# Fifty-one series of extra products in one group of layer 0, at other addresses, orders and widths

## The chip, the cores and the metric

The kernel runs on one core of a Trainium2 chip. The metric is the device time of one execution in microseconds; a smaller time is better. Times of before are the median of two runs, and one further execution was profiled.

## The reference

A small decoder with two layers works on 16 learned prefix tokens and 256 input tokens, T = 272 in all, with a model width of 2048 and a hidden width of 8192. Layer 0 mixes tokens by forgetting attention, layer 1 by stick-breaking attention; after each mixer comes an MLP, and the change lies in that of layer 0:

```python
def squared_relu_mlp(h, w_up, w_down):
    u = h @ w_up
    return jnp.square(jax.nn.relu(u)) @ w_down
...
        h = h + squared_relu_mlp(rms_norm(h, norm_mlp[layer]), w_up[layer], w_down[layer])
```

Only the 256 input tokens are returned, so layer 1 carries 256 columns where layer 0 carries 272.

## The kernel before

Activations are kept feature-major: 128 features on the partitions, tokens along the free dimension. Every weight matrix is cut into groups of 512 output features. A group (`gemm_group`, line 179) has four accumulators in PSUM (`acc`, one for 128 output features each) and runs over four blocks of 512 input features. A block comes in two halves: each is loaded by the queue of SyncE into a tile `raw`, ScalarE copies it into the high part `whi` (line 220), and VectorE subtracts to get the low part `wlo` (line 221). The pools for `raw`, `whi` and `wlo` have four buffers each, which is two blocks.

The activations are split in the same way into a high and a low part (`Split`, line 101). For each chunk of 128 input features and each accumulator there are three products: high weights with high rows, high with low, low with high. In each, 128 columns of weights are the stationary operand and the 272 (or 256) columns of one activation row are the moving operand. All are issued by one helper, `gemm_matmul`, whose products therefore all stand under line 168. It can tie a product to the one before it, so that the order on TensorE is the order of the program.

Places in SBUF are chosen: in layer 0 an activation row starts 192 bytes behind a multiple of 256 bytes (`ROWS`), and the 128 columns of weights at a multiple of 256 bytes. In layer 1 the rows start at a multiple of 256 bytes and the weights 64 bytes behind one, and in some groups three products read 6 columns more (`widen`).

The MLP (`mlp`, line 550) has four quarters f of the hidden width; each has four groups g of `w_up` and then four of `w_dn`. The group of the change is f = 0, g = 1 of layer 0, the 18th group of the program. Its normed rows are called `x_m`, its accumulators `acc`; block 2 is its third. In blocks 1 and 2 the products run through the first half for all four accumulators, then through the second.

A second PSUM pool, `patt` (line 48), has four banks for everything that is not a group's accumulator: scores, transposes, sums of norms. At the start of the program nine products into a tile `idle` of that pool are made while the first loads arrive (line 64); no instruction reads that tile.

Of the kernel before, what the change touches and what calls it, by code (L numbers as in the profile page):

```python
# [9 lines left out]
F32 = mybir.dt.float32  # L10
# [5 lines left out]
P = 128  # L16
# [4 lines left out]
T = M + S  # L21
# [13 lines left out]
def yoco_kernel(ctx: ExitStack, tc: tile.TileContext, hT_in, gains, b_f, w_f, w_qkv0, w_o0, w_up, w_dn,  # L35
# [12 lines left out]
    patt = ctx.enter_context(tc.tile_pool(name="patt", bufs=4, space=bass.MemoryType.PSUM))  # L48
# [117 lines left out]
    def gemm_matmul(*args, **kw):  # L166

        ins = nc.tensor.matmul(*args, **kw).ins  # L168
        if queued and pinned[0]:
            tc.add_manual_dep(ins, queued[0].name, mybir.DependencyInfo(mybir.DependencyClass.NoSync,  # L170
                                                                        mybir.DependencyReason.DATA))
        queued[:] = [ins]
# [3 lines left out]
        tc.add_manual_dep(ins.ins, queued[0].name, mybir.DependencyInfo(mybir.DependencyClass.NoSync,  # L176
                                                                        mybir.DependencyReason.DATA))

    def gemm_group(wblk, sp, t0, evac, before={}, after={}, load_x=None, widen=False):

        uid[0] += 1
        u = uid[0]
        accs = [pacc.tile([P, 512], F32, tag="acc", name=f"acc_{u}_{m}") for m in range(4)]
        n = T - t0
        for kb in range(4):
            src_w = wblk[kb].rearrange("p (k c) -> p k c", k=4)  # L190
            if kb in before:
                before[kb]()
            piece = 1 if load_x is not None and kb < 2 else 2
            raws = [wraw.tile([P, 2, 512], F32, tag="raw", name=f"raw_{u}_{kb}_{hf}") for hf in range(2)]
            for k0 in range(0, 4, piece):
                if load_x is not None:
                    load_x(range(4 * kb + k0, 4 * kb + k0 + piece))
                if load_x is not None and kb == k0 == 0:

                    for c0 in (0, 256):  # L200
                        nc.scalar.dma_start(raws[0][:, 0, c0:c0 + 256], src_w[:, 0, c0:c0 + 256])
                else:
                    nc.sync.dma_start(raws[k0 // 2][:, k0 % 2:k0 % 2 + piece], src_w[:, k0:k0 + piece])
            parts = []
            for hf in range(2):
                whi = wspl.tile([P, 2 * 576], F32R, tag="whi", name=f"whi_{u}_{kb}_{hf}")
                wlo = wspl.tile([P, 2, 576], F32R, tag="wlo", name=f"wlo_{u}_{kb}_{hf}")
                if t0:
                    whi = whi.rearrange("p (k c) -> p k c", k=2)[:, :, 16:528]
                    wlo = wlo[:, :, 16:528]  # L210
                else:
                    whi = whi[:, :1024].rearrange("p (k c) -> p k c", k=2)
                    wlo = wlo[:, :, :512]
                boxes = [(o, piece, 0, 512) for o in range(0, 2, piece)]
                if load_x is not None and kb == hf == 0:
                    boxes[:1] = [(0, 1, 0, 256), (0, 1, 256, 512)]
                for o, no, c0, c1 in boxes:
                    src = raws[hf][:, o:o + no, c0:c1]
                    hp, lp = whi[:, o:o + no, c0:c1], wlo[:, o:o + no, c0:c1]
                    on_act = nc.scalar.activation(hp, src, AF.Copy)  # L220
                    on_dve = nc.vector.tensor_tensor(out=lp, in0=src, in1=hp.bitcast(F32), op=ALU.subtract)  # L221
                parts.append((whi, wlo))
            if kb in after:
                with tc.issue_after(on_act.ins), tc.issue_after(on_dve.ins):
                    after[kb]()


            if load_x is not None and kb == 0:
                runs = [([kc], range(4)) for kc in range(4)]
            elif kb in (0, 3):  # L230
                runs = [(range(4), [m]) for m in range(4)]
            else:
                runs = [(range(2 * hf, 2 * hf + 2), range(4)) for hf in range(2)]
            pinned[0] = load_x is None
            for kcs, ms in runs:
                if t0:
                    series = [(w, x, kc, m) for w, x in ((0, "hi"), (0, "lo"), (1, "hi")) for m in ms for kc in kcs]
                else:
                    series = [(w, x, kc, m) for m in ms for kc in kcs for w, x in ((0, "hi"), (0, "lo"), (1, "hi"))]
                for i, (w, x, kc, m) in enumerate(series):  # L240
                    over = SPAN if widen and kb == m == 0 and i in (0, 4, 8) else 0
                    rhs = sp.wide[x] if over else getattr(sp, x)[:, 4 * kb + kc]
                    gemm_matmul(accs[m][:, :n + over], parts[kc // 2][w][:, kc % 2, m * P:(m + 1) * P], rhs,
                                start=kb == kc == w == 0 and x == "hi", stop=kb == kc == 3 and w == 1)
                if kb == 3:
                    for m in ms:
                        evac(m, accs[m][:, :n])

    def residual_add(c, acc, t0):
        nc.vector.tensor_tensor(out=hT[:, c, t0:], in0=acc, in1=hT[:, c, t0:], op=ALU.add)  # L250
# [6 lines left out]
    def load_x(chunks):  # L257
        c0, n = chunks[0], len(chunks)
        nc.sync.dma_start(hT[:, c0:c0 + n, :], hT_in[:, c0:c0 + n, :])
        if c0 == 0:  # L260
            nc.sync.dma_start(g_sb, gains)
        for c in chunks:
            split_chunk(xa, G_A0, c)

    def first_norm(kb):
        if kb == 1:
            box["wf"] = load_gates()
        for c in range(4 * kb, 4 * kb + 4):
            norm.add(c)
# [173 lines left out]
    for g in range(4):  # L443
# [6 lines left out]
        if g == 0:  # L450

            gemm_group(w_qkv0[0], xa, 0, lambda m, acc, qT=qT: nc.scalar.copy(qT[:, m, :], acc),
                       after={kb: (lambda kb=kb: first_norm(kb)) for kb in range(4)}, load_x=load_x)
# [96 lines left out]
    def mlp(layer, xm, norm, t0, last_evac):  # L550
        box = {}

        def get_rstd():
            box["r"] = norm.finish()

        for f in range(N_FF):
            u = Split(f"u{layer}_{f}", t0)
            for g in range(4):
                def evac(m, acc, g=g):
                    c = 4 * g + m  # L560
                    r = tmp.tile([P, T], F32, tag="relu", name=f"relu_{layer}_{f}_{c}")
                    u2 = tmp.tile([P, T], F32, tag="u2", name=f"u2_{layer}_{f}_{c}")
                    nc.vector.scalar_tensor_tensor(out=r[:, t0:], in0=acc, scalar=0.0, in1=box["r"][:, t0:],
                                                   op0=ALU.max, op1=ALU.mult)
                    nc.scalar.activation(u2[:, t0:], r[:, t0:], AF.Square)
                    nc.scalar.activation(u.hi[:, c], u2[:, t0:], AF.Copy)
                    nc.vector.tensor_tensor(out=u.lo[:, c], in0=u2[:, t0:], in1=u.hi[:, c].bitcast(F32),
                                            op=ALU.subtract)
                gemm_group(w_up[layer, f, g], xm, t0, evac, {2: get_rstd} if f == g == 0 else {},
                           widen=t0 == M and g % 2 == 1)  # L570
            for g in range(4):
                def evac(m, acc, g=g):
                    residual_add(4 * g + m, acc, t0)
                    if f == N_FF - 1:
                        last_evac(4 * g + m)
                gemm_group(w_dn[layer, f, g], u, t0, evac, widen=t0 == M and g % 2 == 1)
# [20 lines left out]
    for g in range(4):  # L597
# [4 lines left out]
        def split_c(kb, g=g):  # L602
            for c in ([4 * kb + g - 1] if g < 3 else [4 * kb + 2, 4 * kb + 3]):
                split_chunk(xc, G_KV, c)

        gemm_group(w_q1[g], xq, M, evac_q1, {2: get_rstd1} if g == 0 else {},
                   after={kb: (lambda kb=kb: split_c(kb)) for kb in range(4)} if g else {}, widen=g > 0)
# [3 lines left out]
    for g in range(4):  # L611
# [4 lines left out]
        s, e, r = (att.tile([P, 4, 416], F32, tag="s", bufs=3, name=f"{t}1_{g}") for t in ("s", "e", "r"))  # L616
# [49 lines left out]
    def last_evac(c):  # L666
        if c < NC - 4:
            normf.add(c)
        else:
            if c == NC - 4:  # L670
                add_squares(normf.acc, True, False)
            sq = tmp.tile([P, T], F32, tag="sq", name=f"sq_fin_{c}")
            nc.scalar.activation(sq[:, M:], hT[:, c, M:], AF.Square)
            add_squares(sq, False, c == NC - 1)
        if c < NC - 4:
            nc.scalar.activation(hT[:, c, M:], hT[:, c, M:], AF.Copy, scale=g_sb[:, G_FIN, c:c + 1])
# [3 lines left out]
    a, y, t, rs = (fin[:, i, :] for i in range(4))  # L680
# [9 lines left out]
    for i in range(2):  # L690
        pr = patt.tile([P, 512], F32, tag="patt", name=f"pr_fin_{i}")
        for b in range(2):
            nc.tensor.matmul(pr[:, b * P:(b + 1) * P], rs[:, b:b + 1].to_broadcast([P, P]), ident,
                             start=True, stop=True)
# [67 lines left out]
```

## Time and profile before

| | us |
|---|---|
| median of the runs (2276.69 and 2277.55) | 2277.12 |
| the profiled execution | 2277.15 |
| its span, first to last instruction | 2275.4 |
| PE busy | 2262.0 |
| DVE busy | 1361.6 |
| ACT busy | 1113.5 |

PE is TensorE's products, PEld its weight loads, DVE is VectorE, ACT ScalarE, POOL GpSimd, and SP the queue of SyncE. L168 is line 168 of the kernel. A product's duration in the profile runs from its start to its modelled end and overlaps that of the next, so the pace of a stream is read from starts or from the number of products in a stretch. Names in the profile leave out buffer numbers. A float32 product has two rows in the profile, and one in lower precision (float32r, as in the groups) has one.

### The profile page before, as it was taken

What the parts mean: (1) busy time and instruction counts of PE and PEld (TensorE: products, weight loads), DVE (VectorE), ACT (ScalarE), POOL (GpSimd) and SP (SyncE); (2) the same over time, 40 slices, a digit from 0 to 9 for tenths busy, and PEclk for the clock granted to TensorE, in tenths of its full rate; (3) what the DMA queues carried; (4) which work ended last, traced back from release to release, by engine and by line L of the source; (5) the groups of instructions that cost most, each with busy time, mean ns of one, the idle gap of its engine ahead of it and who ended that gap; (6) DMA issues with size and microseconds to landing.
All of it is one profiled execution on the core that took longest, in us unless ns stands there. A gap on an engine that the chain in (4) does not pass through costs nothing.

```text
span 2275.4 us, 44753 instructions
## 1 busy us (share of the span) xinstructions
PE 2262.0 (99%) x18882; PEld 2255.5 (99%) x18882; DVE 1361.6 (60%) x1915; ACT 1113.5 (49%) x1536; POOL 28.5 (1%) x75
## 2 busy tenths in 40 slices
PE   9999999999999999999999999999999999999998
PEld 9999999999999999999999999999999999999998
DVE  7767676555454455445666677766555555555554
ACT  6554554443354344344454567655544443544553
POOL 0000000000000000000000000000000000000000
PEclk9999999999999999999999999999999999999999
DMA  7545554555555555555565544455656656556563
GB/s 241 174 162 168 182 168 160 184 179 173 186 170 185 179 170 186 172 185 179 170 192 183 180 160 157 159 187 189 199 187 193 203 187 201 191 188 202 184 204 130
DMA packets 116905, 412.32 MB, mean 181 GB/s; under 512 B 13520, under 2 KB 16992, under 8 KB 116704
## 3 DMA queue, kind: packets, MB, share of 16 engines
q1 hardware_dynamic: 114560, 406.29, 54.7%
q8 instruction: 148, 2.42, 0.4%
q10 hardware_dynamic: 2144, 3.17, 0.4%
q14 instruction: 53, 0.43, 0.1%
HBM read 407.29 MB, written 2.11 MB: 180 GB/s over the span
## 4 chain that ended last, share of the span: by engine, by line
PE 98%; DMA 1%; DVE 0%; ACT 0%; issue 0%; ACTq 0%; SPq 0%; DVEq 0%
PE acc L168 96%; PE po L414 1%; PE ps L345 0%; DMA fk<-f_dram 0%; PE po L417 0%; PE ps L343 0%; DMA raw<-w_qkv 0%; PE po L418 0%; PE pf L293 0%; DVE ob L704 0%; ACTq L319 0%; DVE s L471 0%; PE pms_fin L661 0%; DVE ob L701 0%; ACT x_o L438 0%
## 5 line engine op out<-in xcount | busy, mean ns | idle before, releaser
L221 DVE TENSOR_TENSOR wlo<-raw,whi 128x1024 fp32r<-128x1024 f32 (+1 forms) x773 | 926.5, 1215 | 664.6 <-ACT whi L220 657.2
L220 ACT ACTIVATE whi<-raw 128x1024 fp32r<-128x1024 f32 (+1 forms) x773 | 797.0, 1051 | 934.9 <-PE acc L168 904.8
L168 PE MATMUL acc<-x_u,whi 128*128 128x272 f32 (+1 forms) x4096 | 642.9, 281 | 0.0
L168 PE MATMUL acc<-x_m,whi 128*128 128x272 f32 (+1 forms) x4096 | 642.5, 281 | 0.0
L168 PEld LDWEIGHTS acc<-x_u,whi 128*128 128x128 f32 x4096 | 565.8, 188 | 0.0
L168 PEld LDWEIGHTS acc<-x_m,whi 128*128 128x128 f32 x4096 | 565.7, 188 | 0.0
L168 PE MATMUL acc<-x_u,wlo 128*128 128x272 f32 (+1 forms) x2048 | 440.8, 281 | 0.0
L168 PE MATMUL acc<-x_m,wlo 128*128 128x272 f32 (+1 forms) x2048 | 440.7, 281 | 0.0
L168 PE MATMUL acc<-x_a,whi 128*128 128x272 f32 (+1 forms) x2048 | 353.2, 285 | 0.7 <-ACT whi L220 0.7
L168 PEld LDWEIGHTS acc<-x_u,wlo 128*128 128x128 f32 x2048 | 323.3, 188 | 0.0
L168 PEld LDWEIGHTS acc<-x_m,wlo 128*128 128x128 f32 x2048 | 323.3, 188 | 0.0
L168 PEld LDWEIGHTS acc<-x_a,whi 128*128 128x128 f32 x2048 | 300.0, 188 | 2.2 <-ACT whi L220 1.2
L168 PE MATMUL acc<-x_a,wlo 128*128 128x272 f32 (+1 forms) x1024 | 253.1, 285 | 0.9 <-DVE wlo L221 0.9
L168 PE MATMUL acc<-x_kv,whi 128*128 128x272 f32 x1024 | 192.6, 287 | 0.0
L168 PEld LDWEIGHTS acc<-x_a,wlo 128*128 128x128 f32 x1024 | 175.5, 188 | 2.0 <-DVE wlo L221 1.6
L168 PE MATMUL acc<-x_o,whi 128*128 128x272 f32 (+1 forms) x1024 | 162.5, 282 | 0.7 <-ACT x_o L438 0.4
L168 PEld LDWEIGHTS acc<-x_kv,whi 128*128 128x128 f32 x1024 | 160.1, 188 | 0.0
L168 PE MATMUL acc<-x_kv,wlo 128*128 128x272 f32 x512 | 147.1, 287 | 0.0
L168 PEld LDWEIGHTS acc<-x_o,whi 128*128 128x128 f32 x1024 | 142.0, 188 | 1.4 <-DVE x_o L439 0.7
L250 DVE TENSOR_TENSOR hT<-acc,hT 128x272 f32<-128x272 f32 (+1 forms) x160 | 69.0, 431 | 86.4 <-PE acc L168 86.2
L168 PE MATMUL acc<-x_o,wlo 128*128 128x272 f32 (+1 forms) x512 | 110.5, 282 | 0.0
L168 PEld LDWEIGHTS acc<-x_kv,wlo 128*128 128x128 f32 x512 | 96.5, 188 | 0.0
(187 smaller groups left out, 1053.4 us busy)
## 6 DMA issues: line engine op xcount, KB each, us to landing
raw<-w_up SPq DMA_DIRECT2D x256, 512.0 KB, 4.5
raw<-w_dn SPq DMA_DIRECT2D x256, 512.0 KB, 4.5
raw<-w_qkv SPq DMA_DIRECT2D x92, 512.0 KB, 4.0
raw<-w_o SPq DMA_DIRECT2D x64, 512.0 KB, 4.5
raw<-w_kv SPq DMA_DIRECT2D x64, 512.0 KB, 4.6
raw<-w_q SPq DMA_DIRECT2D x32, 512.0 KB, 4.6
fk<-f_dram ACTq DMA_DIRECT2D x4, 544.0 KB, 6.4
raw<-w_qkv SPq DMA_DIRECT2D x7, 256.0 KB, 4.5
```

The source lines that it names most:

```text
L168: ins = nc.tensor.matmul(*args, **kw).ins
L220: on_act = nc.scalar.activation(hp, src, AF.Copy)
L221: on_dve = nc.vector.tensor_tensor(out=lp, in0=src, in1=hp.bitcast(F32), op=ALU.subtract)
L250: nc.vector.tensor_tensor(out=hT[:, c, t0:], in0=acc, in1=hT[:, c, t0:], op=ALU.add)
L414: ins = nc.tensor.matmul(po[:, i, :], v[:, j, 0, :], p[:, j, :2 * P], start=i == 0, stop=False)
```

## The change

A new helper, `probes`, makes 51 series of products and is called once: in layer 0, in group f = 0, g = 1, after the weights of block 2 have been split and before the products of that block. It takes the first half of the block. The moving operand is read from the high part `whi` (`wa`, 1024 columns in one run), the stationary one is 128 columns of the low part `wlo` (`wb`). Each series writes one tile `push` of the pool `patt`: its first product starts the sum, its last ends it, and no instruction reads it. The result of the kernel doesn't depend on it.

- 28 series of 32 products: from one product to the next the start of the moving operand goes on by `dx` pieces of 64 bytes and that of the weights by `dw`, each modulo four pieces; dx = dw = 0 is left out.
- 8 series of 20: 17 pieces of 16 columns, with a step of 48 or of 32 columns between the pieces, from four starting places.
- 4 series of 20 that read 272 columns backwards, one by one, and 4 that read 17 pieces of 16 columns in backward order.
- 2 series of 20 with the weights at 40 or 24 columns, and 5 with 264, 276, 280, 288 and 304 columns instead of 272.

```diff
+    def probes(parts, u):
+
+        (wa, wb), _ = parts
+        wa, wb = wa.rearrange("p k c -> p (k c)"), wb[:, 0]
+        near = lambda k: wb[:, 16 * k:16 * k + P]
+        row = lambda k, n=T: wa[:, 16 * k:16 * k + n]
+        lines = lambda o, step, n: bass.AP(wa.tensor, wa.offset + o, [wa.ap[0], [step, n], [1, 16]])
+        kinds = []
+        for dx in range(4):
+            for dw in range(4):
+                e = (dx - dw) % 4
+                for first in ((0, 1, 2, 3) if e == 0 else (0, 1) if e == 2 else (0,)):
+                    if dx or dw:
+                        kinds.append((32, [(row((first + i * dx) % 4), near(i * dw % 4)) for i in range(4)]))
+        for step in (48, 32):
+            for k in range(4):
+                kinds.append((20, [(lines(16 * k, step, 17), near(0))]))
+        for k in range(4):
+            kinds.append((20, [(bass.AP(wa.tensor, wa.offset + 16 * k + T - 1, [wa.ap[0], [-1, T]]), near(0))]))
+        for k in range(4):
+            kinds.append((20, [(lines(16 * k + T - 16, -16, 17), near(0))]))
+        for o in (40, 24):
+            kinds.append((20, [(row(3), wb[:, o:o + P])]))
+        for n in (264, 276, 280, 288, 304):
+            kinds.append((20, [(row(3, n), near(0))]))
+        for i, (n, pairs) in enumerate(kinds):
+            t = patt.tile([P, 512], F32, tag="patt", name=f"push_{u}_{i}")
+            for k in range(n):
+                x, w = pairs[k % len(pairs)]
+                c = 1
+                for _, m in x.ap[1:]:
+                    c *= m
+                gemm_matmul(t[:, :c], w, x, start=k == 0, stop=k == n - 1)
...
+            if probe and kb == 2:
+                probes(parts, u)
+
             if load_x is not None and kb == 0:
...
                 gemm_group(w_up[layer, f, g], xm, t0, evac, {2: get_rstd} if f == g == 0 else {},
+                           probe=layer == 0 and f == 0 and g == 1,
                            widen=t0 == M and g % 2 == 1)
```

On TensorE in the program before, at the end of block 1 of that group and the start of block 2 (`acc_0` to `acc_3` are the group's accumulators, `whi_1_1` is the high part of block 1, second half, `whi_2_0` that of block 2, first half; the last column is the output's shape and how often the row repeats):

```order
L168 MATMUL acc_3_5326<-x_m_3910,whi_1_1_5395 128x272 x2
L168 MATMUL acc_3_5326<-x_m_3910,wlo_1_1_5396 128x272
L168 MATMUL acc_0_5323<-x_m_3910,whi_2_0_5451 128x272 x2
L168 MATMUL acc_0_5323<-x_m_3910,wlo_2_0_5452 128x272
...
L168 MATMUL acc_1_5324<-x_m_3910,whi_2_0_5451 128x272 x2
```

The two rows ahead of the first product into `acc_0` are the last of block 1. In the changed program the same place on TensorE begins so, with the first three of the 51 series:

```order
L168 MATMUL acc_3_5326<-x_m_3910,whi_1_1_5395 128x272 x2
L168 MATMUL acc_3_5326<-x_m_3910,wlo_1_1_5396 128x272
L168 MATMUL push_0_5459<-whi_2_0_5451,wlo_2_0_5452 128x272 x32
L168 MATMUL push_1_5492<-whi_2_0_5451,wlo_2_0_5452 128x272 x32
L168 MATMUL push_2_5525<-whi_2_0_5451,wlo_2_0_5452 128x272 x32
```

The series follow block 1 directly. And it ends so, with the four widest series and the first product of block 2 into `acc_0`:

```order
L168 MATMUL push_47_6782<-whi_2_0_5451,wlo_2_0_5452 128x276 x20
L168 MATMUL push_48_6803<-whi_2_0_5451,wlo_2_0_5452 128x280 x20
L168 MATMUL push_49_6824<-whi_2_0_5451,wlo_2_0_5452 128x288 x20
L168 MATMUL push_50_6845<-whi_2_0_5451,wlo_2_0_5452 128x304 x20
L168 MATMUL acc_0_5323<-x_m_3910,whi_2_0_5451 128x272 x2
```

The 1356 products stand in one run between the two blocks; nothing else on TensorE changes its place, and VectorE, ScalarE, GpSimd and SyncE have the same instructions in the same order as before.

More of the change, by code (lines that the diff above doesn't have):

```diff
@@ L177, in behind, with gemm_group @@
                                                                         mybir.DependencyReason.DATA))
-    def gemm_group(wblk, sp, t0, evac, before={}, after={}, load_x=None, widen=False):
+    def probes(parts, u):
[30 more added lines that the diff above has]
+                gemm_matmul(t[:, :c], w, x, start=k == 0, stop=k == n - 1)
+    def gemm_group(wblk, sp, t0, evac, before={}, after={}, load_x=None, widen=False, probe=False):
         uid[0] += 1
```

## The prediction

> **What bounds the kernel now.** The first view is the page: busy times, the granted clock in 40 slices, and the chain that ended last.
>
> ```profile
> PE 2262.0 (99%) x18882; PEld 2255.5 (99%) x18882; DVE 1361.6 (60%) x1915; ACT 1113.5 (49%) x1536; POOL 28.5 (1%) x75
> PEclk9999999999999999999999999999999999999999
> PE 98%; DMA 1%; DVE 0%; ACT 0%; issue 0%; ACTq 0%; SPq 0%; DVEq 0%
> ```
>
> TensorE is busy for 2262.0 of 2275.4 us, the granted clock never drops, and the chain that ends last lies to 98% on PE. So a product added on PE has nothing to hide behind: it moves the end by the time until the next product can start. PEld, the weight loads, is as full as PE; each product of this kernel brings its own weight load.
>
> That time is not the mean of the groups by line (281 to 288 ns): consecutive products overlap, so the step from start to start has to be read. Two views give it: the windows, over long stretches that hold nothing but products of line 168, and the timeline at the place of the change.
>
> ```profile
> 470.00:930.00 460.00, 460.00 (x3732) 1.00 0.55 179
> 1500.00:2200.00 700.00, 700.00 (x6176) 1.00 0.60 193
> ```
>
> The columns are the stretch, its length, PE's busy time with the number of products, granted clock, DMA share and GB/s. The first stretch is layer 0, 272 columns a product: 460.00/3732 = 123.3 ns a step. The second is layer 1 with 256 columns (a few with 262): 700.00/6176 = 113.3 ns.
>
> ```profile
> 452.37 1.23 DVE L221 TENSOR_TENSOR wlo<-raw,whi 128x1024 fp32r<-128x1024 f32 x1 [1.34 <-ACT whi L220]
> ...
> 453.79 0.41 PE L168 MATMUL acc<-x_m,whi 128*128 128x272 f32 x2
> 454.04 0.29 PE L168 MATMUL acc<-x_m,wlo 128*128 128x272 f32 x1
> 454.16 0.41 PE L168 MATMUL acc<-x_m,whi 128*128 128x272 f32 x2
> ```
>
> These rows (start, length, engine) are the place of the change, block 2 of the second group of w_up in layer 0, which starts on PE near 454.16. From 453.79 to 454.16 are three steps in 0.37 us, again 123.3 ns, without a gap.
>
> **The change, part by part.** It removes and moves nothing; VectorE, ScalarE, GpSimd and the transfers keep their instructions in their order. On PE one unbroken run goes in between block 1 and block 2: 28 series of 32 and 23 of 20, 896 + 460 = 1356 products. They read what block 2 needs anyway (its high weights as the moving rows, its low weights as the stationary ones) and write tiles that nobody reads.
>
> *Waits it adds.* The first product waits for the low half of block 2, wlo. The four buffers hold two blocks, so when the row at 452.37 writes a half of block 3, both halves of block 2 are complete; block 2's own third product asked for them 0.25 us later anyhow. Cost 0. From the fifth series on, each takes the PSUM bank of the series four before it and waits for PE's own signal that this one is done; at least 60 products lie between, over 7 us at 123 ns. Behind such a wait the whole of PE would stand, but the signal is long there: 0. Meanwhile ScalarE, VectorE and the weight transfers run ahead until their four buffers are full, then stand still, and go on at PE's pace. Nothing waits for them afterwards, and the head start buys nothing: in the two windows PE has no idle time to win back.
>
> *Price of the ordinary steps.* The 28 series read 272 columns in a row like the group's own products, but their start addresses move by 0 to 3 pieces of 64 bytes from product to product, for rows and weights. The group's products always start in the same piece of 256 bytes. Other places occur in before only as single steps among the scores of attention:
>
> ```profile
> 137.82 0.38 PE L345 MATMUL ps<-kh,qh 128*128 128x272 f32 x1
> 138.04 0.29 PE L345 MATMUL ps<-kl,qh 128*128 128x272 f32 x1
> 138.17 0.28 PE L345 MATMUL ps<-kh,ql 128*128 128x272 f32 x1
> 138.30 0.28 PE L343 MATMUL ps<-kT,qT 128*128 128x144 f32 x1
> ...
> 1447.27 0.28 PE L345 MATMUL ps<-kl,qh 128*128 128x272 f32 x1
> 1447.39 0.29 PE L345 MATMUL ps<-kh,ql 128*128 128x272 f32 x1
> 1447.52 0.41 PE L343 MATMUL ps<-kT,qT 128*128 128x144 f32 x2
> ...
> 1449.49 0.30 PE L345 MATMUL ps<-kl,qh 128*128 128x272 f32 x1
> 1449.62 0.29 PE L345 MATMUL ps<-kh,ql 128*128 128x272 f32 x1
> 1449.75 0.28 PE L168 MATMUL acc<-x_kv,wlo 128*128 128x272 f32 x1
> ```
>
> Steps between such products of 272 columns are 0.13 us (138.04 to 138.17 to 138.30), 0.12 (1447.27 to 1447.39) and 0.13 twice (from 1449.49). Not all places cost the same, and the spread is 120 to 130 ns around the group's 123.3. Since a series runs through several places, I take 126 ns, the middle of 123.3 and the dearer rows, rounded down: 896 x 126 = 112.9 us. Bounds: 896 x 120 = 107.5 and 896 x 130 = 116.5.
>
> [...]
>
> *Price of the other orders.* Sixteen series of 20 read their 272 columns otherwise: eight in pieces of 64 bytes with a step of 192 or 128 bytes, four backwards element by element, four in backward pieces. Before has no such read. The nearest row of the same speed is the group's step (123.3), the dearest single one 130; they may go faster by luck, 120. [...]
>
> ```profile
> 1490.07 0.60 PE L414 MATMUL po<-pt,vt 128*128 128x256 f32 x2
> 1490.50 0.38 PE L417 MATMUL po<-pt,vt 128*128 128x128 f32 x2
> ```
>
> Two products of 256 columns in 0.43 us, 215 ns each, so 272 columns would take 228. I take 128 ns, since the same engine reads the same bytes in whole pieces, and a little above the plain series because more edges of pieces meet the weight loads: 320 x 128 = 41.0 us. Bounds 320 x 120 = 38.4 and 320 x 228 = 73.0.
>
> *The rest.* Two series move the weights by half a piece: 40 x 126 = 5.0 us (4.8 to 5.2). Five series are 264, 276, 280, 288 and 304 columns wide; at 123.3/272 = 0.453 ns a column they are 119.7, 125.1, 126.9, 130.6 and 137.8 ns, together 640.1, times 20 = 12.8 us. By the slope between the two windows, (123.3 - 113.3)/16 = 0.625 ns a column, they are 13.0.
>
> *Sum.* 112.9 + 41.0 + 5.0 + 12.8 = 171.7 us. The profiled execution took 2277.15 us (span 2275.4, 1.75 around it), the median of the runs is 2277.12; the sum stands on either: 2277.1 + 171.7 = 2448.8, say 2449 us. With the low bounds 107.5 + 38.4 + 4.8 + 12.8 = 163.5, 2440.6; with the dear single steps for all 272-wide series 116.5 + 41.6 + 5.2 + 13.0 = 176.3, 2453.4.
>
> **The rivals.**
> *Addresses don't matter.* PE might read rows and weights without either disturbing the other; then every 272-wide series runs at 123.3: 1256 x 123.3 = 154.9, plus 12.8 = 167.7 us, 2445 us. For it speaks that the group's step comes back at once after the scores; against it the 0.13 beside 0.12 in the rows above. It lies inside the range. Chance 0.2. [...]
>
> *Backward reads are slow.* If the four series that go element by element run at half speed, 80 x (228 - 128) = 8.0 us come on top: 2457 us. If all sixteen odd orders do, 320 x 100 = 32.0: 2481 us. Nothing in before speaks for or against. Chances 0.15 and 0.06.
>
> *The end comes no later.* Where the run ends, PE could fall into another rhythm and keep it. A stream can have two rhythms at the same addresses, as layer 1 shows just after an attention step and later:
>
> ```profile
> 1479.50:1489.50 10.00, 10.00 (x88) 1.00 0.49 161
> 1510.00:1520.00 10.00, 10.00 (x91) 1.00 0.74 235
> ```
>
> That is 3% between the two. Behind the place of the change come 15272 products, 7442 of them with 272 columns. To end within 2% of before (45.5 us), these would have to win 171.7 - 45.5 = 126.2 us, 8.3 ns each. But the 256-wide ones already run the better of the two, and 272 columns at the better stream's 113.3/256 x 272 = 120.4 ns would win 7442 x 2.9 = 21.6 us: 2427 us. So this cannot reach the other side; at 0.13 us it would go the other way, 7442 x 6.7 = 49.9 us and 2499 us. Against any shift: all of 460 us holds one rhythm although scores interrupt the stretches before it. Chance 0.03 each way.
>
> *Nothing is run.* Products into unread tiles could be dropped when the program is prepared: 2277 us, no change. Against it stands a tile of the same kind in before, written by nine float32 products (two rows each) that nobody reads, and all are in the trace:
>
> ```profile
> L64 PE MATMUL idle<-mean_w x18: 275/421/579, 1.1 to 4.8; 128*128 128x128 f32 x18
> ```
>
> Chance 0.01.
>
> **How the numbers follow.** The forecast (series between 120 and 130 ns, odd orders alike) has 0.52 and holds 2440.6 to 2453.4. With the first rival and the slow backward series that is 0.87, from 2440.6 to 2457. I widen this to 2440 to 2468, for backward reads at a third of the speed (another 8 to 9 us, 2466) and steps that a series keeps up which single rows do not show. Outside are all sixteen at half speed, both shifts of rhythm and the dropped products: 0.13, with a little left for the unknown. What can be told from no change here is 2%, 45.5 us; every case but the dropped products is above it: slower 0.985, same 0.01, faster 0.005.
>
> **What would show it.** In the page of the changed kernel PE has 18882 + 1356 = 20238 products and stays at 99%, with a new group of products push<-whi,wlo that no one waits for and no idle time before it. In the windows, the run of series should start near 454.2 and take about 172 us, and a stretch behind it, moved by that, should hold again some 3732 products in 460 us; fewer or more would be a new rhythm. In the timeline each series shows its step: the plain ones 120 to 130 ns, in groups by the difference of the two moves if addresses matter, all 123 if not. The backward ones are the weakest number. I would be wrong if one of them stood near 230, if a wait for a bank showed PE idle between series, or if the granted clock fell below full in these slices.

## The result and the profile after

The changed kernel takes 2448.12 us (median of 2447.73 and 2448.52) against 2277.12 us before, 171.0 us more; the ratio is 1.0751 with a 95% interval of 1.0705 to 1.0797. The forecast was 2449 us, between 2440 and 2468.

The page of the changed kernel answers the rows shown of before: busy times, granted clock, transfers in 40 slices, the chain that ended last, and the new group of products.

```profile
PE 2433.7 (99%) x20238; PEld 2427.2 (99%) x20238; DVE 1362.1 (56%) x1915; ACT 1113.5 (46%) x1536; POOL 28.5 (1%) x75
PEclk9999999999999999999999999999999999999999
GB/s 229 174 175 164 172 170 171 99 1 1 122 173 187 174 182 173 181 181 174 181 172 187 192 173 163 164 156 188 192 190 189 195 202 194 191 188 197 197 199 129
PE acc L168 89%; PE push L168 7%; PE po L451 1%; DMA raw<-w_qkv 0%; PE ps L382 0%; DMA fk<-f_dram 0%; PE po L454 0%; PE ps L380 0%; DMA hT<-hT_in 0%; PE po L455 0%; PE pf L330 0%; DVE ob L742 0%; ACTq L356 0%; ACT whi L254 0%; DVE s L508 0%
L168 PE MATMUL push<-whi,wlo 128*128 128x272 f32 (+4 forms) x1356 | 170.7, 289 | 0.0
```

1356 products and 171.7 us of PE are new, with no idle time before them and a full clock. ScalarE and VectorE have the busy times of before; in the slices of the run the transfers stand still (1 GB/s): ScalarE waits 172.42 us for PE's products, and the queue of SyncE 173.1 us for VectorE's next `wlo`. In the chain the series have 7% of the span for themselves: nothing hides them.

The windows of the changed kernel show the run by kinds of series, and a stretch of 460 us behind it:

```profile
454.20:566.60 112.40, 112.40 (x900) 1.00 0.03 12
566.60:586.90 20.30, 20.30 (x163) 1.00 0.00 1
586.90:596.90 10.00, 10.00 (x83) 1.00 0.01 2
596.90:607.00 10.10, 10.10 (x83) 1.00 0.01 2
607.00:612.10 5.10, 5.10 (x43) 1.00 0.00 0
612.10:624.70 12.60, 12.60 (x98) 1.00 0.00 1
...
641.00:1101.00 460.00, 460.00 (x3732) 1.00 0.54 179
```

The six rows are the 28 ordinary series, the pieces with a step, the rows backwards by element, the backward pieces, the weights moved by half a piece, and the widths. A count holds every product of which a part lies in the window, which is some 2 too many; so the ordinary series come to about 112.4/898 = 125.2 ns a step. Summed from start to start over exactly its own products, each kind measures 112.1, 20.3, 10.0, 10.1, 5.0 and 13.0 us, 170.5 us in all. The last row is the stretch at 470 of before, moved by 171 us, and holds the same 3732 products: in this stretch behind the run nothing goes faster or slower.

Product by product, the changed program is 0.06 us early ahead of the run and 170.45 us late behind it, and this stays so for 8000 products. Then 0.22 us come on top in layer 1: near 1495 us of before, behind an attention step, some 50 products of the changed program run at 117.8 ns where those of before have 113.3 already. The span is longer by 171.4 us; most of what is left lies in the last eight products of the program (row of before, then of after):

```profile
L693 PE MATMUL pr_fin<-ident,fin 128*128 128x128 f32 x8 | 1.2, 288 | 1.3 <-DVE fin L687 1.3
```

```profile
L731 PE MATMUL pr_fin<-ident,fin 128*128 128x128 f32 x8 | 2.1, 441 | 1.3 <-DVE fin L725 1.3
```

They wait for the final norm, and in the run of after they took 2.1 instead of 1.2 us. In e7 and e8 below they took 1.2 us again, although series were added there too, so this is not a price of the series.

### The profile page after: what moved, and what is told of

Its sections match the earlier page's. It is cut to its first block, busy times and chain, and to the rows that moved or that the text cites. A ratio compares the mean times of both kernels' runs of the same rounds, so it can differ in the third digit from the quotient of the medians.

```text
span 2446.8 us, 47465 instructions
## 1 busy us (share of the span) xinstructions
PE 2433.7 (99%) x20238; PEld 2427.2 (99%) x20238; DVE 1362.1 (56%) x1915; ACT 1113.5 (46%) x1536; POOL 28.5 (1%) x75
## 4 chain that ended last, share of the span: by engine, by line
PE 98%; DMA 1%; DVE 0%; ACT 0%; issue 0%; ACTq 0%; DVEq 0%; SPq 0%
PE acc L168 89%; PE push L168 7%; PE po L451 1%; DMA raw<-w_qkv 0%; PE ps L382 0%; DMA fk<-f_dram 0%; PE po L454 0%; PE ps L380 0%; DMA hT<-hT_in 0%; PE po L455 0%; PE pf L330 0%; DVE ob L742 0%; ACTq L356 0%; ACT whi L254 0%; DVE s L508 0%
## 5 line engine op out<-in xcount | busy, mean ns | idle before, releaser
L168 PE MATMUL push<-whi,wlo 128*128 128x272 f32 (+4 forms) x1356 | 170.7, 289 | 0.0
L168 PEld LDWEIGHTS push<-whi,wlo 128*128 128x128 f32 x1356 | 170.6, 188 | 0.0
```

## The experiments

In all of them `probes` stands for the helper of the change; the result of the kernel doesn't depend on what it makes. Where a step is read from the timeline, a row gives the start, the length of a merged stretch and its number of products; the step is (length - 0.29)/(number - 1), as one product's row is 0.29 us long. Steps "from the starts" leave out the first few products of a series, where it follows on the one before.

**One place for all (e1).**

```diff
+        kinds = [(n, [(row(3), near(0))]) for n, _ in kinds]
```

> All 1356 products read 272 columns from one place, that of the group's own products (rows 192 bytes, weights 0 bytes behind a multiple of 256). Theory (each product costs PE its own step, and the step follows from the addresses): 1356 x 123.3 = 167.2 us, 2444.3 us in all, and the step is the same at the run's start, where ScalarE, VectorE and the transfers are still at work, and at its end, where they stand still. Rival (the traffic of the other engines makes part of the step): it falls towards 120 ns once they stand still, some 163 us, 2440 us.

Measured: 2443.71 us. The windows of this kernel with all engines, one in the run and one behind it:

```profile
456.00:616.00 160.00, 160.00 (x1300) 160.00 (x1299) 0.00 (x0) 0.00 (x0) 0.00 (x0) 1.00 0.01 4
641.00:801.00 160.00, 160.00 (x1300) 160.00 (x1299) 80.35 (x93) 65.04 (x78) 0.00 (x0) 1.00 0.51 179
```

The columns behind PE and PEld are DVE, ACT and POOL. In the run they are idle, behind it they work and 179 GB/s arrive: 1300 products in 160 us both times. The other engines' traffic is no part of the step, and the rival falls. The run is 167.24 us, 1356 x 123.3, which also gives the price of the places, orders and widths together: 170.5 - 167.2 = 3.3 us.

**One bank (e2).**

```diff
+        t = patt.tile([P, 512], F32, tag="patt", name=f"push_{u}")
         for i, (n, pairs) in enumerate(kinds):
-            t = patt.tile([P, 512], F32, tag="patt", name=f"push_{u}_{i}")
```

> The 51 series write one tile, so that the waits for a bank are gone; addresses as in the change. Theory (the waits are over long before they are asked for): 2448.1 us, every step as in the change. Rival (a wait holds PE up by 0.1 us although its signal is there): 47 waits less, 4.7 us less, 2443.4 us.

Measured: 2446.81 us. The run is 170.51 us as in the change, to 10 ns, so 47 waits cost nothing, and the rival falls. The 1.3 us that this kernel is shorter lie ahead of the run: its first series starts at 452.82 us instead of 454.10, since PE stands still a little less in the first 75 us (near 75 us one step is 0.68 instead of 1.21 us).

**A bank for each product (e9).**

```diff
-            t = patt.tile([P, 512], F32, tag="patt", name=f"push_{u}_{i}")
             for k in range(n):
+                t = patt.tile([P, 512], F32, tag="patt", name=f"push_{u}_{i}_{k}")
...
-                gemm_matmul(t[:, :c], w, x, start=k == 0, stop=k == n - 1)
+                gemm_matmul(t[:, :c], w, x, start=True, stop=True)
```

> The 1356 products of the change with their addresses, but each is a sum of its own in the next of the four banks, so that it waits for the product four before it instead of the series four before. Theory (a product's row in the profile is 288 ns long and four steps are 500 ns, so the signal is still there in time): steps as in the change, 170.5 us, 2448 us. Rival (the signal comes later than the profiled end, after some 600 ns or more): four steps can't be shorter than that, 150 ns a step or more, 2481 us or more.

Measured: 2446.96 us in one run, 170.47 us for the series. Even a wait for the product four before is over in time, and the rival falls. How much nearer it could come was not tried.

**Half the weights (e3).**

```diff
-                gemm_matmul(t[:, :c], w, x, start=k == 0, stop=k == n - 1)
+                gemm_matmul(t[:64, :c], w[:, :64], x, start=k == 0, stop=k == n - 1)
```

> Each product loads 64 columns of weights instead of 128 and so makes 64 output rows; rows and their places as in the change. [...]

Measured: 2445.80 us, and a run of 169.5 us. Loads of the change and of this kernel, by tile:

```profile
L168 PEld LDWEIGHTS push<-whi,wlo x1356: 187/188/194, 454.0 to 624.3; 128*128 128x128 f32 x194
```

```profile
L168 PEld LDWEIGHTS push<-whi,wlo x1356: 133/134/138, 452.3 to 621.6; 128*64 128x64 f32 x194
```

The load is 54 ns shorter for 64 columns less, 0.84 ns a column, yet the mean step fell by 0.7 ns only, from 125.7 to 125.0: with 272 columns the step does not go with the size of the load, and it is not the load that it waits for. The sum is nearly that of the change, but some series did change: the 23rd fell from 128.4 to 123.9 ns, the 13th rose from 123.2 to 124.9. So half the load shifts single series by some 2 to 5 ns and the mean by 0.7. "Surplus", in the expectations of e6 and e7, is what a step has over a bare stream of columns. How long that is for 272 columns no run shows; the lowest average of a series of 272 columns is 118.6 ns (e6).

**Fixed places (e4).**

```diff
+        for dx in range(4):
+            for dw in range(4):
+                kinds.append((40, [(row(dx), near(dw))]))
+        for k in range(4):
+            kinds.append((40, [(row(k, 256), near(0))]))
```

> 16 series of 40 products of 272 columns, each with one place for rows (0 to 3 pieces of 64 bytes) and one for weights (0 to 3), and four series of 40 with 256 columns, weights at 0; 800 products instead of 1356. Theory (what matters is how far the place of the rows is from that of the weights): four classes by the difference, the one at 3 with 123.3 ns, the others 124 to 129, and the same at 256 columns, where a difference of 3 has 113.3; some 640 x 125.5 + 160 x 116 = 98.9 us, 2376 us. Rival (the place of the rows alone matters): classes by rows, no change with that of the weights.

Measured: 2374.69 us in one run. The timeline of this kernel inside six of its series: rows and weights at 0 and 0; 0 and 3; 1 and 0; 3 and 0; then 256 columns at 0 and 0 and at 3 and 0.

```profile
452.53 4.30 PE L168 MATMUL push<-whi,wlo 128*128 128x272 f32 x33
...
467.55 4.34 PE L168 MATMUL push<-whi,wlo 128*128 128x272 f32 x33
...
472.48 4.47 PE L168 MATMUL push<-whi,wlo 128*128 128x272 f32 x34
...
512.75 4.24 PE L168 MATMUL push<-whi,wlo 128*128 128x272 f32 x33
...
532.81 4.12 PE L168 MATMUL push<-whi,wlo 128*128 128x256 f32 x33
...
547.05 3.90 PE L168 MATMUL push<-whi,wlo 128*128 128x256 f32 x33
```

That is 125.3, 126.6, 126.7, 123.4, 119.7 and 112.8 ns by the rows, and 125.3, 126.7, 126.7, 123.3, 120.0 and 113.3 from the starts. All sixteen combinations fall into classes by the difference of rows and weights, modulo four pieces: 125.3 to 125.4 at 0, 126.7 at 1, 126.6 to 126.7 at 2, and 123.3 at 3, whatever the places themselves. At 256 columns the differences 0 to 3 cost 120.0, 117.8, 118.7 and 113.3 ns. The theory of the difference holds, the rival of the rows alone falls. The group's own products stand at 3, the cheapest class.

That holds for places which stay from product to product. In the change both places also move together in some series, so that their difference stays though the places don't. Two of these series, both with moves of two pieces, at a difference of 0 and then of 3:

```profile
514.79 3.25 PE L168 MATMUL push<-whi,wlo 128*128 128x272 f32 x25
...
526.16 3.79 PE L168 MATMUL push<-whi,wlo 128*128 128x272 f32 x29
```

From the starts, these moves cost 123.3 ns at differences 0, 1 and 2 and 125.3 at 3, so that the class that is cheapest at rest is here the dearest. So the difference within a product is not the whole rule; what of the products before it counts was not tried.

**Sizes of the load (e5).**

```diff
+        for m in (128, 64, 32, 16):
+            for k in range(4):
+                kinds.append((24, [(row(k), wb[:, :m])]))
...
-                gemm_matmul(t[:, :c], w, x, start=k == 0, stop=k == n - 1)
+                gemm_matmul(t[:w.shape[-1], :c], w, x, start=k == 0, stop=k == n - 1)
```

> 16 series of 24 products of 272 columns: rows at 0 to 3 pieces of 64 bytes, weights at 0, loads of 128, 64, 32 and 16 columns (and as many output rows). 384 products instead of 1356. Theory (rows and weight load hinder each other once a step, at a moment that the places set; the size of the load doesn't matter as long as there is one): four classes by place at every size, near 125.3, 126.6, 126.6 and 123.3 ns, and the mean of all near 125, 48.0 us, 2325 us. [...]

Measured: 2324.73 us in one run, 47.9 us for the series. With 128 columns the classes are there again (125.3, 126.8, 126.4, 123.3). With 64 columns they are gone already (123.9 to 124.5), and with 32 the four places cost 123.6 to 125.0, in no like order. With 16 the four places are alike, here rows at 0 and at 3 in the timeline:

```profile
489.76 2.40 PE L168 MATMUL push<-whi,wlo 128*16 128x272 f32 x18
...
498.61 2.40 PE L168 MATMUL push<-whi,wlo 128*16 128x272 f32 x18
```

(2.40 - 0.29)/17 = 124 ns, and 124.2 to 124.5 from the starts for all four. The theory is half right: the step stays at 124 to 125 ns down to a load of an eighth, as it said, but the classes go.

**One element (e6).**

```diff
+        one = lambda t, k, n: t[:, 16 * k:16 * k + 1].to_broadcast([P, n])
+        for k in range(4):
+            kinds.append((24, [(one(wa, k, T), near(0))]))
+        for k in range(4):
+            kinds.append((24, [(row(k), one(wb, 0, P))]))
+        for k in range(4):
+            kinds.append((24, [(one(wa, k, T), one(wb, 0, P))]))
```

> 12 series of 24 products of 272 columns, in which the rows read one and the same element 272 times, or the weights one and the same element 128 times, or both, with the rows' piece at 0 to 3 and the weights' at 0; 288 products. The outputs of the series hold other sums, which nobody reads. Theory (rows and loads hinder each other where they read the same piece of 256 bytes at the same time): with both fixed, the series whose pieces are the same is far dearer than the other three (over 135 ns against 113 to 117), and with one fixed the four places cost the same. Rival (the surplus comes from the step from one piece to the next in the rows alone): fixed rows cost 113 to 116 ns at every place, fixed weights 123 to 127 as ever. Some 288 x 121 = 35 us, 2312 us, by both.

Measured: 2312.59 us in one run. The timeline: fixed rows with ordinary weights, ordinary rows with fixed weights, and both fixed, each on an element of its own tile, in the same piece of 64 bytes modulo 256.

```profile
454.63 2.18 PE L168 MATMUL push<-whi,wlo 128*128 128x272 f32 x17
...
466.05 2.29 PE L168 MATMUL push<-whi,wlo 128*128 128x272 f32 x17
...
477.97 2.18 PE L168 MATMUL push<-whi,wlo 128*128 128x272 f32 x17
```

Steps of 118, 125 and 118 ns (118.6, 124.7 and 118.6 from the starts), and within half a nanosecond the same at every place of the rows. Two operands that stay in the same piece cost no more than in different ones, so the theory of a clash in one piece is wrong. Rows that run through 272 columns cost 6 ns more than rows that stand still, so far the rival is right, though no run shows its 113 to 116 ns at 272 columns (nor the theory's 113 to 117), 118.6 being the least; but with fixed weights the classes of place are gone, and that it had not said. What is left: about 118.6 ns for 272 columns with rows that stand still, about 6 more for rows that run through their columns, and -1 to +2 by how the rows lie to a full load that runs through its columns as well. Rows that stand still also have one value in all columns; whether the address or the value saves the 6 ns was not separated.

**Steps in the weights (e7).**

```diff
+        at = lambda o, *steps: bass.AP(wb.tensor, wb.offset + o, [wb.ap[0], *steps])
+        for n in (T, 256):
+            for step in (2, 3, 4):
+                for k in range(4):
+                    kinds.append((24, [(row(k, n), at(0, [step, P]))]))
```

> 24 series of 24 products, 272 and 256 columns, rows at 0 to 3 pieces, and weights that are read with a step of 2, 3 or 4 columns; 576 products, whose outputs hold other columns. Theory (where rows and load meet sets the surplus): the load passes 2 to 4 times as many pieces in the same time, so the classes change, and one of the 24 may be better than the best so far, 123.3 ns at 272 columns and 113.3 at 256; near 288 x 125 + 288 x 117 = 69.7 us, 2347 us. Rival (the places at the start alone matter): the same four classes as with a step of 1, at 272 columns 125.3, 126.6, 126.6 and 123.3, at 256 columns 120.0, 117.8, 118.7 and 113.3.

Measured: 2377.37 us in one run, 30 us more than forecast. The timeline at 272 columns with steps of 2, 3 and 4, rows at 0:

```profile
452.85 2.40 PE L168 MATMUL push<-whi,wlo 128*128 128x272 f32 x18
...
465.10 3.28 PE L168 MATMUL push<-whi,wlo 128*128 128x272 f32 x18
...
482.05 4.37 PE L168 MATMUL push<-whi,wlo 128*128 128x272 f32 x18
```

124 ns for the first; in the other two a product's own row is longer than 0.29 us, so the starts are better: 173.2 and 233.7 ns. Over all places these two steps cost 173.2 to 176.6 and 233.3 to 233.7 ns, and at 256 columns much the same (173.3 to 175.2 and 233.3). So there the step follows the weights and not the rows, 233.3/128 = 1.82 ns a column of weights where the load in e3 has 0.84; this is what the forecast of 69.7 us lacked, the series took 101.8. The theory let the load pass more pieces in the same time, which steps of 3 and 4 do not bear out; why they are so dear and a step of 2 is not was not shown. The classes changed, as the theory said: with a step of 2 the rows at 0 to 3 cost 124.5, 126.2, 124.6 and 127.4 ns, and at 256 columns 120.0 to 120.8. So the rival's four classes fall, but no step was better than 123.3 or 113.3 ns, which the theory had hoped for.

**Widths (e8).**

```diff
+        for k in (3, 0):
+            for n in (128, 192, 224, 240, 248, 252, 256, 260, 264, 268, 272, 276, 280, 284, 288):
+                kinds.append((24, [(row(k, n), near(0))]))
```

> 30 series of 24 products with 15 widths from 128 to 288 columns, rows at 3 and at 0 pieces, weights at 0; 720 products. Theory (a step can't be shorter than the weight load, whose last columns end some 0.84 ns each after the first): below some 250 columns the step stops falling, at 107 to 112 ns; above that it rises by more than the columns, 113.3 at 256, 120.0 at 264, 123.3 at 272 with rows at 3. Rival (a step goes with the width alone): 0.453 ns a column, 58 ns at 128 columns. By the theory about 720 x 117 = 84 us, 2361 us, by the rival 720 x 114 = 82 us.

Measured: 2361.97 us in one run, 86.6 us for the series. The timeline, rows at 3, for 128, 224, 252 and 256 columns:

```profile
452.68 2.06 PE L168 MATMUL push<-whi,wlo 128*128 128x128 f32 x17
...
458.08 2.07 PE L168 MATMUL push<-whi,wlo 128*128 128x224 f32 x17
...
466.25 2.20 PE L168 MATMUL push<-whi,wlo 128*128 128x252 f32 x17
...
469.11 2.09 PE L168 MATMUL push<-whi,wlo 128*128 128x256 f32 x17
```

From the starts: 111.7 to 111.8 ns at 128, 192 and 224 columns; 113.3 at 256, but 120.0 at 252 and 260, 123.3 at 268 and 272, 126.6 at 276. The rival falls, and the floor that the theory forecast is there. That it is the load's floor is argued and not shown, as no run made the load smaller at these widths. The rise is no line: with rows at 3, 4 columns less than 256 cost 6.7 ns more. With rows at 0 they don't: 116.6 ns at 252, 119.4 at 256, 118.5 at 260.

**One series in layer 1 (e10).**

```diff
+        kinds = [(32, [(wa[:, 0, 16:272], wb[:, 0, :P])])]
...
-                           probe=layer == 0 and f == 0 and g == 1,
+                           probe=layer == 1 and f == 0 and g == 1,
```

> Instead of the run in layer 0, one series of 32 products of 256 columns in the same group of layer 1, rows one piece of 64 bytes ahead of the weights' place (modulo 256 bytes); the group's own products stand at three. Theory (PE keeps a rhythm that a disturbance leaves behind until another one ends it, as layer 1 showed with 117.8 ns after an attention step): the 32 cost 117.8 each, 3.8 us, and the 288 products behind them up to the next group with wider products run at 117.8 instead of 113.3 ns, 1.3 us more; 2282 us. Rival (each product's step follows from its own place): 113.3 ns right after the series, 2281 us. The trace tells the two apart, not the time.

Measured: 2282.64 us in one run. The windows: before the series, twice behind it, and after the next group with wider products.

```profile
1587.50:1597.50 10.00, 10.00 (x90) 1.00 0.52 169
1602.00:1612.00 10.00, 10.00 (x87) 1.00 0.41 129
1612.00:1622.00 10.00, 10.00 (x87) 1.00 0.40 123
1650.00:1660.00 10.00, 10.00 (x90) 1.00 0.46 139
```

From the starts, the step is 113.3 ns before the series, 117.8 in all 288 products behind it, and 113.3 again once the next group has begun with its wider ones. The theory holds: at these addresses PE keeps the rhythm it was left in. The rival falls. What sets such a rhythm stays open: in layer 0 the series of 256 columns at a difference of 3 fell to 113.3 ns at once behind one of 118.7 (e4).

## Why the prediction was right

*The bound.* That a product on PE moves the end by its own step held to 0.1 us: the run takes 170.51 us, and what was 0.06 us early ahead of it is 170.45 us late behind it. What the other engines gain by running ahead buys nothing, as said.

*The waits* were put at 0 and cost 0 (e2, and e9 with a far shorter margin).

*The sum* was 171.7 us against 170.5 us in the run:

| term | forecast, us | measured, us |
|---|---|---|
| 28 ordinary series | 112.9 (126 ns) | 112.1 (125.1 ns) |
| 16 other orders | 41.0 (128 ns) | 40.4 (126.3 ns) |
| weights moved by half a piece | 5.0 | 5.0 |
| widths | 12.8 | 13.0 |

That the measured time, 171.0 us more, fits a little better is chance: 0.2 us of another rhythm in layer 1 and 0.8 us in the last eight products, neither in the sum, came on top in the profiled execution.

The single steps among the scores of attention, 120 to 130 ns, bracket the series: the ordinary ones average from 123.2 to 128.4 ns. The middle value of 126 was 0.9 ns too high; inside these series single steps go from 119 to 135 ns, so that a single row says little of a series. Nor do the series fall into groups by the difference of the two moves, as the prediction had it among its signs: with a difference of 2 they reach from 123.2 to 128.4 ns. For the other orders 128 ns was near, but its reason, edges of pieces that meet the weight loads, is not borne out: with half the load (e3) the twelve series in pieces still cost 126.4 ns on average instead of 126.8. Widths at a fixed rate per column were right in the sum and not one by one: 288 columns cost 133.5 ns where the rate gave 130.6.

*Addresses don't matter* (2445 us) is wrong, though its time is only 3 us away: e1 against the change is 3.3 us of run for places, orders and widths, and e4 has the classes. The time alone could not have told the two apart, as the stretch ahead of the run already differs by 1 to 2 us among these executions. With a load of 16 columns (e5, 124.2 to 124.5 ns at all four places) or one operand at rest (e6, 118.6 with fixed rows and 124.7 with fixed weights) there are no classes; with both running through their columns there are (e4, 123.3 to 126.7 ns).

*Backward reads are slow* is wrong: by element they cost 124.4 to 125.3 ns, on average 124.8 and no more than the ordinary series. The price of a slow read, 228 ns, rested on a misreading: the two rows at 1490.07 are one float32 product, which has two rows, so that 256 columns took 0.43 us in all and 215 ns a row. No run shows rows read at that price. It bore on this rival and on the upper bound only.

*The rhythm* was a real effect at the wrong place. In layer 0 the run leaves nothing behind: 3732 products in 460 us as before. In layer 1 a single series of 32 leaves 4.5 ns on each of 288 products (e10). So the rival was rightly kept as a case, and its low chance was right for this place only.

*Nothing is run* is ruled out by the 20238 products in the page.

## What to carry to other kernels

When one engine is busy through the whole span and the chain of waits lies on it (PE here, 99% and 98%), an addition costs its count times the step from start to start, read from a long window of like instructions; the mean duration in the groups (288 ns here against steps of 123) is of no use for that. The places of rows and weights in SBUF are worth some 3% of a product's step here (123.3 to 126.7 ns, e4). Where they stayed from product to product, the difference of the two was what to set, not each one; where they moved, the classes were others (123.3 and 125.3 ns with moves of two pieces) and have to be measured. After a stretch of other products, look whether the old step comes back: at 272 columns it did at once (3732 products in 460 us), at 256 only behind the wider products of the next group, after 288 products at 117.8 ns (e10).

## What the runs showed that was not expected

- Two operands that each read one element all the time cost 118.6 ns whether their places agree or not, while both running through their columns make classes from 123.3 to 126.7 ns by the difference of their places, and other classes when the places move. Why 272 running columns cost 6 ns more than one repeated was not settled, nor what makes the classes.
- With rows at 3 a step at 252 columns is dearer than at 256 (120.0 and 113.3 ns).
- Weights with a step of 3 or 4 columns cost some 173 and 233 ns a product, at 272 as at 256 columns of rows (e7).
- At 256 columns PE has two lasting rhythms at the same addresses, 113.3 and 117.8 ns; at 272 columns the stretch behind the run showed no second one.
